# A transformer layer with windowed attention and mLSTM: values by direction, queries split in the projections, output weights loaded over items 8 to 13

## The chip, the cores and the metric

The kernel runs on one core of a Trainium2 chip. The metric is the device time of one execution in microseconds; the time of a kernel is the median of its runs. The engines are named as in the profile: PE (TensorE, with its weight loads PEld), DVE (VectorE), ACT (ScalarE), POOL (GpSimd) and SP, which issues the DMAs.

## What is computed

One layer over 1024 latent tokens of width 1024 with a prefix of 256 context tokens. Both are normed and modulated, go through one input projection, and feed two head groups: grouped attention over a band of 128 positions, all context keys and a sink, and a bidirectional mLSTM in four heads. Both are joined in one output projection; a gated feed-forward follows. Cut to its core:

```python
px = modulate(rms_norm(x, g_pre_mix), sh_m, sc_m) @ w_in
aqx, akx, avx, mqx, mkx, mvx, mox, mgx = split(px)
att_x = window_attention(rope(aqx), rope(akx), avx, kc, vc, sink)  # p = exp(s - m) * inv;  p @ v
...
num = einsum('bhts,bhsv->bhtv', s, vc) + w_inter * einsum('bhvd,bhtd->bhtv', C, qc)
den = s.sum(-1) + w_inter * einsum('bhd,bhtd->bht', n, qc)
h = num / maximum(abs(den), exp(-m_t))      # forward and backward, summed
...
mix_x = concatenate([att_x, ml_x], -1) @ w_out
x = x + gt_m * rms_norm(mix_x, g_post_mix)
x = x + gt_f * rms_norm(swiglu(modulate(rms_norm(x, g_pre_ffn), ...)), g_post_ffn)
```

## The kernel before

Matmuls that must be exact to float32 are made as three: every operand is split into a high part (a cast, on ACT) and a low part (a subtraction, on DVE or POOL), and `mm3` adds high x high, high x low and low x high. The stages stand one after the other in the trace: modulation vectors, norm and transposed tokens (0 to 162 us), projections (162 to 307), attention and mLSTM (307 to 498), output projection (to about 590) and feed-forward.

**Projections.** `TILES` lists 13 tiles of 128 output rows: mLSTM keys and queries (mk, mq), attention keys (ak), attention queries (aq0 to aq3), output gates (mo). `tproj` makes one tile with 48 matmuls of 512 columns (three accumulators where the context needs one, all of tag "mm", four banks of PSUM), and its result is evicted by `conv`, `rope` or a sigmoid while PE makes the next tile. aq tiles are stored to DRAM (`aq_d`) as float32.

**Attention and mLSTM.** There are 16 items (n, g): a block of 128 query positions and a key head. `Soft(i)` makes the scores (`scores(h)`: four matmuls into a tile of tag "s", two banks each and two of them; DVE's L780 then evicts, masks and takes the row's limit) and `norm` (exponentials on ACT, L789; a reciprocal on DVE; the scaling on POOL, L794). `Values(i)` transposes the probabilities (`tr`, L808, into a bank "pt"), splits them (`th` on ACT, `tl` on DVE) and multiplies them with the values into one bank "po" (`mm`, L818 and L819; `out` copies and adds). In items 0 to 7 block n = i of the mLSTM is made too: `ml_scores` (L693, in tag "s"), `ml_values`, `ml_norm`, `ml_out`. The two halves of a 128-row mLSTM query tile hold two heads (hb = 0 and 1). A call of `ml_values` takes one direction d and one half hb: one bank, for each of two heads a matmul of 64 rows with the state (L707) and one of 128 rows with the values (L708), then two small operations and a reciprocal on DVE (L711 to L713) and two evictions (ACT L717 for d = 0, DVE L719 for d = 1). Scores run two items ahead of values.

The strings `PLAN_ML` and `PLAN` set the order in which an item's steps are written. A scheduler then orders the instructions of each engine from that, by its own estimates, up to the last two items, which stand under a manual order. PSUM has three banks of tag "pt" and one of "po". `q_load(i)` fetches the queries of an item, `q_split` (POOL, L570 and L571) makes their high and low parts.

**Output weights.** `wout_load(j)` loads one of eight 128 x 1024 slabs of w_out, casts it on ACT (L749) and makes the low part on POOL (L750); j = 0 is made in two halves on ACT and DVE. They lie in tiles `R(k)` of a shared pool, the high part in R(2j), the low part in R(2j+1) and the raw slab in R(2j-1). `omm(n, hf, ks)` multiplies row n's split mix (`msplit`, mh and ml) with the slabs 4 hf + k; 24 matmuls for one half of a row.

Of the kernel before, what the change touches and what calls it, by code (L numbers as in the profile page):

```python
# [9 lines left out]
F32 = mybir.dt.float32  # L10
# [6 lines left out]
P = 128  # L17
# [16 lines left out]
PLAN_ML = "T0 q A0 A1 A2 A3 T1 T2 T3 M0 M1 T4 V0 N0 M2 V1 M3 M4 O z V2 w V3 s N1 x"  # L34
PLAN = "T0 q A0 A1 A2 A3 T1 T2 T3 N0 M0 T4 M1 M2 N1 M3 M4 O z l"


def body(tc, x, ctx, vecs, bcv, bada, gqm, gqf, wada, ws1, ws2, wt, wout, wfi, wfo,
# [377 lines left out]
    aq_d = tc.dram_tile([8, 64, S], F32, name="aq_d")  # L416
# [140 lines left out]
    qds, qhl, prs, wo = {}, {}, {}, {}  # L557

    def q_load(i):

        n, g = items[i]
        qd = qds[i] = qq.tile([P, 4, P], F32, name="qd", tag="qd", bufs=2)
        for d in range(2):
            dma(qd[64 * d:64 * d + 64], aq_d[4 * g:4 * g + 4, :, n * P:(n + 1) * P].rearrange("h d t -> d h t"))

    def q_split(i):
        qd = qds.pop(i)
        qh = qq.tile([P, 4, P], F32R, name="qh", tag="qh", bufs=2)
        ql = qq.tile([P, 4, P], F32R, name="ql", tag="ql", bufs=2)
        pool.tensor_scalar(qh, qd, 1.0, 1.0, MUL, MUL)  # L570
        pool.tensor_tensor(ql, qd, qh.bitcast(F32), SUB)  # L571
        qhl[i] = qh, ql
# [16 lines left out]
    for j, name in enumerate(TILES):  # L589
# [25 lines left out]
        elif name.startswith("aq"):  # L615
            t = T(0, f"aq{i}")
            rope(ps, t, 0.125)
            for g in range(2):
                dma(aq_d[4 * g + i], t[64 * g:64 * g + 64])
        else:  # L620
            t = R(14 if i == 3 else 15, "so", (S,))
            for k in range(2):
                act.activation(t[:, k * 512:(k + 1) * 512], ps[k], AF.Sigmoid)
            dve.tensor_scalar(t, t, vec[:, VGML + i:VGML + 1 + i], None, MUL)
            dma(so_d[i], t)
        if name in rest:
            ada_rest(rest[name], j + 1)
        if name == "aq3":
# [3 lines left out]
            for i in range(2):  # L632
                q_load(i)
                q_split(i)
# [28 lines left out]
    qa = atp[1]  # L663
    qa.tile([P, 80], F32, name="padq")

# [34 lines left out]
    def ml_values(n, d, hb):  # L700
        wt_, qp_, hs = wts[n], qps[n], hss[n][0]
        s_, r0 = rows_of(n, d)
        cs = state(d, s_)
        r = slice(hb * 64, hb * 64 + 64)
        pv = bank().rearrange("p a b -> p (a b)")[:, 0:258].rearrange("p (j v) -> p j v", j=2)
        for j in range(2):
            pe.matmul(pv[:, j, :], qp_[r, d, j, :], cs[r, j, :], start=True, stop=False)  # L707
            pe.matmul(pv[:, j, :], wt_[:, d, 2 * j + hb, :], V[:, n, 2 * j + hb, :], start=False, stop=True)  # L708
        dn = qa.tile([P, 2], F32, name="dn", tag="dn", bufs=8)
        den = pv[:, :, 128]  # L710
        dve.tensor_tensor(dn, den, emcol[:, r0 + hb:r0 + 4:2], MAX)  # L711
        dve.scalar_tensor_tensor(dn, den, -1.0, dn, MUL, MAX)
        dve.reciprocal(dn, dn)  # L713
        for j in range(2):
            t = hs[:, 2 * j + hb]
            if d == 0:
                act.activation(t, pv[:, j, 0:128], AF.Copy, scale=dn[:, j:j + 1])  # L717
            else:
                dve.scalar_tensor_tensor(t, pv[:, j, 0:128], dn[:, j:j + 1], t, MUL, ADD)  # L719
# [18 lines left out]
    def wout_load(j):  # L738
        h, l = R(2 * j, f"woh{j}", (D,), F32R), R(2 * j + 1, f"wol{j}", (D,), F32R)
        if j == 0:  # L740
            for i in range(2):
                sl = slice(i * 512, (i + 1) * 512)
                load_split(h[:, sl], l[:, sl], wout[j][:, sl],
                           qq.tile([P, 4, P], F32, name="wor0", tag="qd", bufs=2).rearrange("p a b -> p (a b)"))
            wo[j] = h, l
            return
        raw = R(2 * j - 1, f"wor{j}", (D,))
# [83 lines left out]
    for i in range(2):  # L831
# [5 lines left out]
        if i == 0:  # L837
            q_load(2)
            ml_scores(0)

    for i in range(NIT):
# [6 lines left out]
        for k in (PLAN_ML if i < NT else PLAN).split():  # L848
            op, n = k[0], int(k[1:] or 0)
            if op == "q" and a:  # L850
                q_split(i + 2)
            elif op == "w" and i + 1 < NT:
# [11 lines left out]
            elif op == "V" and i < NT:  # L864
                ml_values(i, n // 2, n % 2)
# [6 lines left out]
            elif op == "l" and i > NT:  # L872
                for j in {9: (7,), 10: (6,), 11: (5, 4), 12: (3, 2), 13: (1, 0)}[i]:
                    wout_load(j)

# [3 lines left out]
    ops_ = {0: pb.tile([P, 1024], F32, name="s", tag="s", bufs=2)}  # L879
    mhl = {}  # L880

    def msplit(n, hf):
        h, l = (qq.tile([P, 4, P], F32R, name=f"m{x_}{hf}", tag=f"q{x_}", bufs=2) for x_ in "hl")
        split(h, l, mix[n][:, 4 * hf:4 * hf + 4, :])
        mhl[n, hf] = h, l

    def omm(n, hf, ks):
        h, l = mhl[n, hf]
        for k in ks:
            j = 4 * hf + k  # L890
            for i in range(2):
                sl = slice(i * 512, (i + 1) * 512)
                mm3(ops_[n][:, sl], (h[:, k], l[:, k]), (wo[j][0][:, sl], wo[j][1][:, sl]), j == 4, j == 3)

# [20 lines left out]
    msplit(0, 0)  # L915
# [4 lines left out]
    omm(0, 0, range(4))  # L920
# [856 lines left out]
```

## Time and profile before

| what | us |
|---|---|
| runs | 1230.72, 1234.12, 1235.18 (median 1234.12) |
| profiled execution | 1231.71 |
| its span | 1229.9 |
| granted TensorE clock, mean | 0.996 |

Times in rows of the profile are counted from the span's start. A row of the timeline has the start, the duration, the engine, the line, the operation, out<-in with shapes and how many like it were merged; what stands in brackets is how long the engine had been idle before and what released it. Matmul rows overlap, since they are pipelined, so what one costs is the time from its start to the start of the next.

### The profile page before, as it was taken

What the parts mean: (1) busy time and instruction counts of PE and PEld (TensorE: products, weight loads), DVE (VectorE), ACT (ScalarE), POOL (GpSimd) and SP (SyncE); (2) the same over time, 40 slices, a digit from 0 to 9 for tenths busy, and PEclk for the clock granted to TensorE, in tenths of its full rate; (3) what the DMA queues carried; (4) which work ended last, traced back from release to release, by engine and by line L of the source; (5) the groups of instructions that cost most, each with busy time, mean ns of one, the idle gap of its engine ahead of it and who ended that gap; (6) DMA issues with size and microseconds to landing.
All of it is one profiled execution on the core that took longest, in us unless ns stands there. A gap on an engine that the chain in (4) does not pass through costs nothing.

```text
span 1229.9 us, 16238 instructions
## 1 busy us (share of the span) xinstructions
PE 1193.5 (97%) x5859; PEld 968.9 (79%) x5859; DVE 799.9 (65%) x1385; ACT 578.1 (47%) x1105; POOL 205.8 (17%) x245
## 2 busy tenths in 40 slices
PE   7889999999999998999999999999999999999997
PEld 1779878877777776887778888888888888888886
DVE  3882177772877788446867677767777755554567
ACT  3754533211766786587643333334333334444443
POOL 0651410235544476000000000000000000000000
PEclk9899999999999999999999999999999999999999
DMA  8542854556533320522034465575645548665853
GB/s 313 168 132 70 280 188 144 181 145 191 153 90 87 112 78 10 188 86 86 18 104 136 180 218 198 204 246 195 230 141 177 176 162 279 205 205 188 299 188 129
DMA packets 91096, 202.30 MB, mean 164 GB/s; under 512 B 9092, under 2 KB 29956, under 8 KB 89608
## 3 DMA queue, kind: packets, MB, share of 16 engines
q1 hardware_dynamic: 91016, 201.27, 49.4%
q8 instruction: 46, 0.75, 0.2%
q14 instruction: 34, 0.28, 0.1%
HBM read 149.85 MB, written 50.73 MB: 163 GB/s over the span
## 4 chain that ended last, share of the span: by engine, by line
PE 78%; DMA 7%; DVE 7%; POOL 3%; ACT 3%; issue 2%; SPq 1%; DVEq 0%; POOLq 0%; ACTq 0%
PE xv L72 8%; PE xv L70 8%; PE xv L71 8%; PE pt L70 5%; PE pt L71 5%; PE pt L72 5%; PE pt L708 2%; PE pt L707 2%; PE pt L808 2%; DMA wb<-in_wada 2%; PE op L72 2%; PE fx L70 2%; PE fx L71 2%; PE fx L72 2%; PE op L71 2%
## 5 line engine op out<-in xcount | busy, mean ns | idle before, releaser
L59 DVE TENSOR_TENSOR fo<-fr,fo 128x1024 fp32r<-128x1024 f32 x77 | 92.7, 1222 | 70.9 <-ACT fo L58 67.7
L58 ACT CAST fo<-fr 128x1024 fp32r<-128x1024 f32 x77 | 79.5, 1050 | 74.0 <-PE pt L72 34.9
L441 PE MATMUL t<-hh,th 128*128 128x512 f32 x208 | 82.5, 397 | 1.8 <-ACT cr L458 1.8
L442 PE MATMUL t<-hl,th 128*128 128x512 f32 x208 | 82.1, 395 | 0.0
L1192 ACT CAST wS<-wr 128x512 fp32r<-128x512 f32 x88 | 54.1, 622 | 55.8 <-PE pt L72 37.5
L1194 DVE TENSOR_TENSOR wS<-wr,wS 128x512 fp32r<-128x512 f32 x88 | 60.3, 688 | 20.7 <-ACT wS L1192 20.7
L444 PE MATMUL t<-hh,tl 128*128 128x512 f32 x208 | 68.2, 393 | 0.0
L70 PE MATMUL xv<-tT,wS 128*128 128x512 f32 x168 | 66.0, 393 | 0.0
L72 PE MATMUL xv<-tT,wS 128*128 128x512 f32 x168 | 65.6, 391 | 0.0
L71 PE MATMUL xv<-tT,wS 128*128 128x512 f32 x168 | 65.5, 390 | 0.0
L492 DVE SCALAR_TENSOR_TENSOR acc<-wb,csil,acc 128x1024 f32<-128x1024 f32 x24 | 33.9, 1411 | 40.6 <-DMA wb<-in_wada 40.6
L441 PEld LDWEIGHTS t<-hh,th 128*128 128x128 f32 x208 | 39.1, 188 | 10.4 <-ACT cr L458 2.4
L944 DVE TENSOR_TENSOR wr<-wr 128x512 f32<-128x512 f32 x66 | 45.5, 689 | 1.4
L442 PEld LDWEIGHTS t<-hl,th 128*128 128x128 f32 x208 | 39.1, 188 | 8.1 <-issue 1.2
L1226 ACT ACTIVATE es<-es 128x512 f32<-128x512 f32 x22 | 13.9, 633 | 66.6 <-DVE es L947 66.6
L72 PE MATMUL op<-woh,ml 128*128 128x512 f32 x112 | 43.8, 391 | 0.8 <-DVE ml L59 0.8
L444 PEld LDWEIGHTS t<-hh,tl 128*128 128x128 f32 x208 | 38.3, 188 | 7.9 <-issue 1.0
L70 PE MATMUL op<-woh,mh 128*128 128x512 f32 x112 | 44.2, 395 | 0.0
L71 PE MATMUL op<-wol,mh 128*128 128x512 f32 x112 | 43.7, 390 | 0.0
L70 PE MATMUL pt<-fo 128*128 128x512 f32 x110 | 42.8, 389 | 0.0
L71 PE MATMUL pt<-fo 128*128 128x512 f32 x110 | 42.8, 389 | 0.0
L72 PE MATMUL pt<-fo 128*128 128x512 f32 x110 | 42.8, 389 | 0.0
(991 smaller groups left out, 3489.9 us busy)
## 6 DMA issues: line engine op xcount, KB each, us to landing
wr<-in_wfi SPq DMA_DIRECT2D x44, 512.0 KB, 4.8
wb<-in_wada SPq DMA_DIRECT2D x24, 512.0 KB, 4.3
s_d<-a SPq DMA_DIRECT2D x22, 512.0 KB, 6.6
bt<-in_wfo SPq DMA_DIRECT2D x44, 256.0 KB, 3.7
tb_d<-bt SPq DMA_DIRECT2D x11, 1024.0 KB, 4.1
fr<-s_d SPq DMA_DIRECT2D x44, 256.0 KB, 4.5
fr<-tb_d SPq DMA_DIRECT2D x44, 256.0 KB, 4.3
fr<-a_d SPq DMA_DIRECT2D x33, 256.0 KB, 4.2
```

What stands on the lines that cost most here:

```text
L58: act.copy(hi, raw)
L59: dve.tensor_tensor(lo, raw, hi.bitcast(F32), SUB)
L70: pe.matmul(ps, a[0], b[0], start=first, stop=False, **kw)
L71: pe.matmul(ps, a[0], b[1], start=False, stop=False, **kw)
L72: pe.matmul(ps, a[1], b[0], start=False, stop=last, **kw)
L441: pe.matmul(o, wh[:, kt], m[0], start=f, stop=False)
L442: pe.matmul(o, wh[:, kt], m[1], start=False, stop=False)
L444: pe.matmul(o, wl[:, kt], m[0], start=False, stop=l)
L492: dve.scalar_tensor_tensor(a, t, csil[:, kt, 0:1], a, MUL, ADD)
L944: dve.tensor_tensor(out, a, b, SUB)
L1192: act.copy(w[:, 0], raw)
L1194: dve.tensor_tensor(w[:, 1], raw, w[:, 0].bitcast(F32), SUB)
```

## The change

1. Attention queries are split in the projections: each aq tile is cast on ACT and subtracted on DVE, both parts are stored (four stores and not two), and `q_load` makes four loads in place of two, with three buffers. `q_split` is gone from POOL.
2. The context accumulator of `tproj` takes a bank of tag "tp" and not a third one of "mm". In the attention stage "pt" and "po" are allocated first, so that "s" gets other banks than those that the last projection sums hold.
3. `ml_values` takes a direction, with both halves: two banks at once, four state matmuls, four value matmuls, one reciprocal.
4. `wout_load` runs j = 0 to 7 over items 8 to 13, with the raw slab in R(2j+2) (that of j = 7 in V), and all low parts on POOL.
5. `msplit(0, 0)` and `omm(0, 0, ...)` move from the end of the manual order into item 13.

```diff
-PLAN_ML = "T0 q A0 A1 A2 A3 T1 T2 T3 M0 M1 T4 V0 N0 M2 V1 M3 M4 O z V2 w V3 s N1 x"
-PLAN = "T0 q A0 A1 A2 A3 T1 T2 T3 N0 M0 T4 M1 M2 N1 M3 M4 O z l"
+PLAN_ML = "T0 A0 A1 A2 A3 T1 T2 T3 M0 M1 T4 V0 N0 M2 M3 M4 O z V1 w s N1 x"
+PLAN = "T0 A0 A1 A2 A3 T1 T2 T3 N0 M0 T4 M1 M2 N1 M3 M4 O z l"
+PLAN13 = "T0 A0 A1 A2 A3 m T1 T2 P0 T3 N0 M0 T4 M1 P1 M2 N1 M3 P2 M4 O P3 l"
+WLOADS = {8: (0, 1), 9: (2,), 10: (3,), 11: (4,), 12: (5, 6), 13: (7,)}
...
-        ps = [pa.tile([P, 512], F32, name=f"t{j}_{i}", tag="mm", bufs=4) for i in range(3 if with_ctx else 2)]
+        ps = [pa.tile([P, 512], F32, name=f"t{j}_{i}", tag="mm", bufs=4) for i in range(2)]
+        if with_ctx:
+            ps.append(pa.tile([P, 4, P], F32, name=f"tc{j}", tag="tp", bufs=2).rearrange("p a b -> p (a b)"))
...
-        pool.tensor_scalar(qh, qd, 1.0, 1.0, MUL, MUL)
-        pool.tensor_tensor(ql, qd, qh.bitcast(F32), SUB)
-        qhl[i] = qh, ql
+        qhl[i] = [qq.tile([P, 4, P], F32R, name=f"q{p}", tag=f"q{p}", bufs=3) for p in "hl"]
+        for t, src in zip(qhl[i], aq_d):
+            for d in range(2):
+                dma(t[64 * d:64 * d + 64].bitcast(F32), src[4 * g:4 * g + 4, :, n * P:(n + 1) * P].rearrange("h d t -> d h t"))
...
             rope(ps, t, 0.125)
-            for g in range(2):
-                dma(aq_d[4 * g + i], t[64 * g:64 * g + 64])
+            qp2 = R(3, f"aqh{i}", (S,), F32R), t.bitcast(F32R)
+            split(*qp2, t)
+            for d, o in zip(aq_d, qp2):
+                for g in range(2):
+                    dma(d[4 * g + i], o[64 * g:64 * g + 64].bitcast(F32))
...
+    for x_, n in (("pt", 3), ("po", 1)):
+        pb.tile([P, 4, P], F32, name=x_, tag=x_, bufs=n)
...
-    def ml_values(n, d, hb):
+    def ml_values(n, d):
...
-        pv = bank().rearrange("p a b -> p (a b)")[:, 0:258].rearrange("p (j v) -> p j v", j=2)
+        pv = [bank().rearrange("p a b -> p (a b)")[:, 0:258].rearrange("p (j v) -> p j v", j=2) for hb in range(2)]
         for j in range(2):
-            pe.matmul(pv[:, j, :], qp_[r, d, j, :], cs[r, j, :], start=True, stop=False)
-            pe.matmul(pv[:, j, :], wt_[:, d, 2 * j + hb, :], V[:, n, 2 * j + hb, :], start=False, stop=True)
...
+            for hb in range(2):
+                r = slice(hb * 64, hb * 64 + 64)
+                pe.matmul(pv[hb][:, j, :], qp_[r, d, j, :], cs[r, j, :], start=j == 0, stop=False,
+                          skip_group_check=j > 0)
+        for hb in range(2):
+            for j in range(2):
+                pe.matmul(pv[hb][:, j, :], wt_[:, d, 2 * j + hb, :], V[:, n, 2 * j + hb, :], start=False, stop=True,
+                          skip_group_check=j > 0)
...
-        raw = R(2 * j - 1, f"wor{j}", (D,))
+        raw = R(2 * j + 2, f"wor{j}", (D,)) if j < 7 else V.rearrange("p n h v -> p (n h v)")[:, 0:D]
...
+            elif op == "m":
+                msplit(0, 0)
+                ops_[0] = pb.tile([P, 1024], F32, name="op", tag="s", bufs=2)
+            elif op == "P":
+                omm(0, 0, range(n, n + 1))
...
-    msplit(0, 0)
...
-    omm(0, 0, range(4))
```

How this stands on the engines after the scheduler, at three places. Lines after the change are a few higher: L707 and L708 are L711 and L715, L808 is L811, L818 and L819 are L821 and L822, L570/L571 have no successor, L794 is L797.

PE, the values of one direction of an mLSTM item, before (pt is a bank, cs the state, qp the queries, wl the weighted scores):

```order
L707 MATMUL pt_3579<-cs2_2339,qp4_3453 128x129
L708 MATMUL pt_3579<-V_87,wl4_3451 128x129
L707 MATMUL pt_3579<-cs2_2339,qp4_3453 128x129
L708 MATMUL pt_3579<-V_87,wl4_3451 128x129
L819 MATMUL po_3498<-tl__3554,av2_90 128x512
L818 MATMUL po_3498<-th__3562,av2_90 128x512
L707 MATMUL pt_3597<-cs2_2339,qp4_3453 128x129
L708 MATMUL pt_3597<-V_87,wl4_3451 128x129
```

The same place after the change, an item on:

```order
L821 MATMUL po_3680<-th__3734,av2_90 128x512
L711 MATMUL pt_3760<-cs2_2358,qp5_3646 128x129 x2
L715 MATMUL pt_3760<-V_87,wl5_3644 128x129 x2
L822 MATMUL po_3680<-tl__3735,av2_90 128x512
L821 MATMUL po_3680<-th__3743,av2_90 128x512
L711 MATMUL pt_3761<-cs2_2358,qp5_3646 128x129 x2
L715 MATMUL pt_3761<-V_87,wl5_3644 128x129 x2
L822 MATMUL po_3680<-tl__3744,av2_90 128x512
```

Within a bank the two state matmuls now stand together and the two value matmuls too. The banks of the two halves are not interleaved, though the code writes them so: the scheduler has put each bank's four matmuls in one place.

POOL, at the start of the attention stage, before (pr are the probabilities of an item, its first column filled from the sinks in bcr):

```order
L767 COPY pr__2799<-bcr 128x4
L570 TENSOR_SCALAR qh<-qd 128x512
L571 TENSOR_TENSOR ql<-qd,qh 128x512
L794 TENSOR_SCALAR pr__2713<-pr__2713,sm 128x512 x4
L570 TENSOR_SCALAR qh<-qd 128x512
L571 TENSOR_TENSOR ql<-qd,qh 128x512
L794 TENSOR_SCALAR pr__2762<-pr__2762,sm 128x512 x2
```

And after:

```order
L770 COPY pr__2788<-bcr 128x4
L770 COPY pr__2825<-bcr 128x4
L797 TENSOR_SCALAR pr__2736<-pr__2736,sm 128x512 x4
L797 TENSOR_SCALAR pr__2788<-pr__2788,sm 128x512 x2
L770 COPY pr__2984<-bcr 128x4
```

Nothing stands between the copies of the sinks and the first scaling any more.

PE, at the end of the manual order, before (s holds the first row of the output projection here, mh and ml are the split mix, woh and wol the output weights):

```order
L818 MATMUL po<-th__4990,av_90 128x512
L819 MATMUL po<-tl__4991,av_90 128x512
L70 MATMUL s<-woh_4866,mh_4981 128x512
L71 MATMUL s<-wol_4867,mh_4981 128x512
L72 MATMUL s<-woh_4866,ml_4982 128x512
```

These rows go on to 24 matmuls. After the change, item 13 has this, with the same matmuls under the name op:

```order
L822 MATMUL po<-tl__4716,av_90 128x512
L811 MATMUL pt<-cst,pr__4525 128x128 x4
L72 MATMUL op<-woh_4297,mh_4784 128x512
L73 MATMUL op<-wol_4298,mh_4784 128x512
L74 MATMUL op<-woh_4297,ml_4785 128x512
```

22 of the 24 follow each other there, ahead of six transposes of pr__4525, and the last two come eight rows later. Behind the last L822 of the program the second row of the output projection follows at once.

More of the change, by code (lines that the diff above doesn't have):

```diff
@@ L839, in body, with msplit, omm @@
             ml_scores(0)
+    ops_, mhl = {}, {}
+    def msplit(n, hf):
+        h, l = (qq.tile([P, 4, P], F32R, name=f"m{x_}{hf}", tag=f"q{x_}", bufs=3) for x_ in "hl")
+        split(h, l, mix[n][:, 4 * hf:4 * hf + 4, :])
+        mhl[n, hf] = h, l
+    def omm(n, hf, ks):
+        h, l = mhl[n, hf]
+        first, last = (0, 7) if n == 0 else (4, 3)
+        for k in ks:
+            j = 4 * hf + k
+            for i in range(2):
+                sl = slice(i * 512, (i + 1) * 512)
+                mm3(ops_[n][:, sl], (h[:, k], l[:, k]), (wo[j][0][:, sl], wo[j][1][:, sl]), j == first, j == last)
     for i in range(NIT):
@@ L847, in body @@
             break
[L848 removed]
+        for k in (PLAN_ML if i < NT else PLAN13 if i == NIT - 3 else PLAN).split():
             op, n = k[0], int(k[1:] or 0)
[L850 to L852 removed]
+            if op == "w" and i + 1 < NT:
                 ml_load(i + 1)
```

63 lines of the change are left out of this document (19 added, 44 removed).

## Prediction

> **What bounds the kernel now.** I read the page first, for which engine the chain of waits runs over, then the windows by stage, then single rows of the stages that the change touches.
>
> ```profile
> span 1229.9 us, 16238 instructions
> PE 1193.5 (97%) x5859; PEld 968.9 (79%) x5859; DVE 799.9 (65%) x1385; ACT 578.1 (47%) x1105; POOL 205.8 (17%) x245
> ...
> PE 78%; DMA 7%; DVE 7%; POOL 3%; ACT 3%; issue 2%; SPq 1%; DVEq 0%; POOLq 0%; ACTq 0%
> ```
>
> TensorE is busy in all but 36 us of the span, and the chain that ended last is mostly PE. So a change can gain only by giving PE fewer or cheaper instructions, or by taking its few waits. The windows say where other engines are near too (PE, PEld, DVE, ACT, POOL busy, each with its count):
>
> ```profile
> 162.00:307.00 145.00, 143.24 (x763) 114.79 (x761) 91.89 (x132) 33.00 (x48) 40.58 (x60) 1.00 0.55 164
> 307.00:322.00 15.00, 12.21 (x82) 10.04 (x80) 12.45 (x34) 12.12 (x27) 7.99 (x11) 1.00 0.68 223
> 353.00:368.00 15.00, 14.94 (x90) 11.72 (x90) 11.29 (x38) 9.55 (x28) 6.21 (x8) 1.00 0.32 88
> 440.00:484.00 44.00, 39.69 (x250) 33.09 (x251) 40.54 (x88) 38.59 (x88) 36.79 (x39) 1.00 0.11 31
> ```
>
> The projections (162 to 307) and a middle mLSTM item (353 to 368, about one item) are PE alone: DVE has 3.7 us of 15 free. Items 8 to 13 (about 440 to 484) are shared by four engines. Out projection and feed-forward, from 504 on, are not changed, so a gain before them passes to the end whole. The sum below is made against the profiled execution's own 1231.71 us (span 1229.9); the median of the three runs is 1234.12, 2.4 more.
>
> **Values by direction.** This is the largest term, and only the shape of PE's rows makes it. One call of before issues a 64-row state matmul, a 128-row V matmul, and both again (a merged row of x2 is one matmul of the program, in two passes):
>
> ```profile
> 354.32 0.49 PE L707 MATMUL pt<-cs,qp 64*128 64x129 f32 x2
> 354.73 0.49 PE L708 MATMUL pt<-V,wl 128*128 128x129 f32 x2
> 355.15 0.49 PE L707 MATMUL pt<-cs,qp 64*128 64x129 f32 x2
> 355.57 0.49 PE L708 MATMUL pt<-V,wl 128*128 128x129 f32 x2
> 355.81 0.47 PE L819 MATMUL po<-tl__3201,av 128*128 128x512 f32 x1
> ```
>
> From start to start an L707 or L708 takes 0.42 us while a matmul of the other shape follows, and the last L708 takes 0.24 us, since L819 has 128 rows too. The 0.18 us between is what a change of row count costs. The weight loads show it: the load below begins at 354.73, with its own matmul and not ahead of it, whereas between equal shapes the load of L778 begins at 356.13, 0.22 ahead of its matmul at 356.35.
>
> ```profile
> 354.73 0.30 PEld L708 LDWEIGHTS pt<-V,wl 128*128 128x128 f32 x2
> ...
> 356.13 0.19 PEld L778 LDWEIGHTS s<-k,qh 128*128 128x128 f32 x1
> ```
>
> A call has 4 such changes (into L707, to L708, back, to L708). The order after has, for each bank, two 64-row and then two 128-row matmuls: 2 changes. So 2 x 0.18 = 0.36 us a call, and 2 directions x 2 halves x 8 items = 32 calls: 11.5 us of PE's slots. It is not all taken off: item 0 runs beside other waits (PE 12.2 of 15 in 307 to 322), and DVE, ACT and the wait for the scores set some moments once PE is faster. I take five sixths, **-9.6 us**. The bounds are 0 and 13.
>
> The code alternates the row halves (hb 0, 1, 0, 1), and before has rows that show such pairs:
>
> ```profile
> 325.26 0.72 PE L693 MATMUL s<-mq,mk 64*128 64x128 f32 x8
> 325.91 0.44 PE L778 MATMUL s<-k,qh 128*128 128x384 f32 x1
> ```
>
> Four matmuls of alternating halves take 0.65 us, 0.16 each. But the order after puts a bank's four matmuls together, so the two 64-row ones that are neighbours are of one half. I count nothing for pairs.
>
> DVE loses one reciprocal per direction (0.15 us), 0.3 an item; POOL loses two instructions per item. Neither engine binds there, so I count zero. The price of it is in the rivals: a direction's results are read only when both banks are full.
>
> **Projections.** The third accumulator of the context tiles leaves the four "mm" banks. This is the one wait it removes; ACT still evicts mk0's sum when mk1 wants a bank:
>
> ```profile
> 164.31 0.50 PE L441 MATMUL t<-hh,th 128*128 128x512 f32 x1 [1.76 <-ACT cr L458]
> ...
> L58 ACT CAST fo<-fr 128x1024 fp32r<-128x1024 f32 x77 | 79.5, 1050 | 74.0 <-PE pt L72 34.9
> L59 DVE TENSOR_TENSOR fo<-fr,fo 128x1024 fp32r<-128x1024 f32 x77 | 92.7, 1222 | 70.9 <-ACT fo L58 67.7
> ```
>
> The "tp" banks are idle by then. The window had 143.24 of 145.00 us of PE busy, and this wait is the whole rest, so 1.76 us go: **-1.8**. Added: four splits of aq, each a cast (1.05 by the L58 row) and a subtraction (1.22), 4.2 us on ACT and 4.9 on DVE in 145 us, where ACT has 33.0 and DVE 91.9; and 8 more stores and 2 more loads per item on SP. PE hides them, unless an eviction that PE needs is queued behind a split; then up to 2.3 us (1.05 + 1.22) come back. I take 0.
>
> **Start of attention.** Scores no longer take the banks that the last projection sum holds, and POOL no longer splits queries ahead of the first norm:
>
> ```profile
> 308.27 0.75 DVE L624 TENSOR_SCALAR so<-so,vec 128x1024 f32<-128x1024 f32 x1 [6.56 <-ACT so L623]
> 308.38 0.36 PE L778 MATMUL s<-k,qh 128*128 128x256 f32 x1 [1.04 <-ACT so L623]
> ...
> 309.24 0.75 DVE L780 CUSTOM_DVE_ANT_0 pr__2713<-s,mask,bcr 128x512 f32<-128x512 f32 x1 [0.21 <-DMA wl<-w_dr]
> ...
> 311.44 0.62 POOL L570 TENSOR_SCALAR qh<-qd 128x512 fp32r<-128x512 f32 x1 [7.20 <-PE s L778]
> 312.14 1.28 POOL L571 TENSOR_TENSOR ql<-qd,qh 128x512 fp32r<-128x512 f32 x1
> ...
> 314.15 0.55 PE L808 MATMUL pt<-cst,pr__2713 128*128 128x128 f32 x3 [1.03 <-POOL pr__2713 L794]
> ```
>
> The wait of 1.04 goes, but DVE's `so` at 308.27, which still needs that sum's sigmoid, stands ahead of the first L780, so little of it is won: 0.2. The transposes at 314.15 wait 1.03 for a norm that could not begin before 313.42, because two split instructions held POOL from 311.44. They go; DVE's row sums are next, so I take 0.7 of the 1.03. Together **-0.9** (bounds -2.1 and 0).
>
> **Items 8 to 13.** Before, ACT's casts of output weights run early; four of seven whole ones and two halves of 0.62 lie after 427, now all eight:
>
> ```profile
> L749 ACT CAST woh<-wor x7: 1043/1045/1047, 413.8 to 451.1; 128x1024 fp32r<-128x1024 f32 x7
> ...
> L571 POOL TENSOR_TENSOR ql<-qd,qh 128x512 fp32r<-128x512 f32 x3 | 3.9, 1304 | 0.1
> L750 POOL TENSOR_TENSOR wol<-wor,woh 128x1024 fp32r<-128x1024 f32 x7 | 16.8, 2404 | 0.7 <-PE pt L707 0.7
> ```
>
> That is 4 x 1.05 - 1.2, and 0.6 for the moved cast of mh: 3.6 us more on ACT, which has 38.6 of 44. POOL gives up its splits and takes one more L750 of 2.4. Each cast waits for the L750 ahead of it, as h_j lies in raw_j-1; behind a waiting cast on ACT stand the exponentials and the casts of p, and PE waits for those. Bounds 0 and 3.6; I take **+1**.
>
> **End of the stage.** PE's waits between 470 and 490 are these:
>
> ```profile
> PE po L819 <- DVE tl__4825 L59: 1.2, 1, 1.2
> PE po L819 <- DVE tl__4729 L59: 0.8, 1, 0.8
> PE pt L808 <- DVE tl__4807 L59: 0.8, 1, 0.8
> PE po L818 <- DVE mix L827: 0.7, 1, 0.7
> PE s L70 <- ACT mh L58: 0.5, 1, 0.5
> ...
> 497.95 0.39 PE L819 MATMUL po<-tl__4991,av 128*128 128x512 f32 x1
> 498.18 0.39 PE L70 MATMUL s<-woh,mh 128*128 128x512 f32 x1
> ...
> 498.38 0.58 ACT L826 COPY o<-po 64x512 f32<-64x512 f32 x1 [1.73 <-PE po L819]
> 498.98 1.14 ACT L58 CAST mh<-mix 128x512 fp32r<-128x512 f32 x2
> ...
> 503.62 0.39 PE L70 MATMUL op<-woh,mh 128*128 128x512 f32 x1
> ```
>
> The waits are 4.0 us in all. The 24 matmuls of omm(0, 0) now fill 498.18 to 503.62, 0.227 us each. The order after sets them into item 13, 22 of them as one lump of 5 us ahead of its last transposes, and DVE no longer does j=0's low part; I count 3.5 us of the waits covered. In the tail they covered the last copy: the last po matmul ends at 498.34, o takes to 498.96 and the first mh half of 1.14, so PE would go on at 499.6 and not at 498.2. That is 1.4, and with mix and ml, which DVE makes behind the same copy, I estimate 1.8 given back: **-1.7** (bounds -4 and +1).
>
> **Sum.** -1.8 - 0.9 - 9.6 + 1.0 - 1.7 = -13.0: 1218.7 from the profiled execution, 1221.1 from the median. I put down 1220.0, between the two.
>
> **Rivals.** (1) Only half is won, since another thing binds as soon as PE's slots shrink. For it: DVE has 11.3 of 15 us in an item, so it would be at 11 of 13.8, with every L711 still behind PE; ACT is nearly full in items 8 to 13. Against it: PE was busy for 14.94 of the 15 us, so nothing bound beside it yet. Half of 9.6 and all of the 3.6: 1218.7 + 4.8 + 2.6 = 1226.1, 1228.5 from the median. The same 4.8 would be lost if two 64-row loads of one half did not hide behind each other (0.18 of the 0.36 a call): 1223.5; no row of before has that pair.
>
> [...]
>
> (2) Pairs run side by side after all. Per direction that makes the four state matmuls 0.65 for 0.96 and leaves 2 changes of shape for 4, and with the exit it is about 0.85 us; 16 directions x 0.85 x 5/6 = 11 more: 1207.4. Against it stands the order of the banks.
>
> (3) Slower: held banks. Two of the three pt banks belong to a direction until DVE and ACT have read both. Before, the last L708 ends near 356.06 and a bank came free only after these:
>
> ```profile
> 356.09 0.16 DVE L711 TENSOR_TENSOR dn<-pt,emcol 128x2 f32<-128x2 f32 x1 [1.57 <-PE pt L708]
> 356.66 1.15 ACT L717 ACTIVATE hs<-pt,dn 128x128 f32<-128x128 f32 x4 [1.78 <-PE pt L708]
> ```
>
> That is to 357.81, about 1.75 us. If PE stood through it in each of 16 directions, with the scores (1.2 us) covering it in half of them, it would lose 8 x 1.75 + 8 x 0.55 = 18.4 and, with 13.0 won, end at 1237.1; and with no cover at 1246.7. It outweighs the gain from 0.8 us a direction. I price it at 1242. Against it: a third bank is left, and items have some 10 us outside the values for five transposed tiles.
>
> **How the numbers follow.** Forecast 0.60 (1213 to 1227), half won 0.25 (1223 to 1231), pairs 0.07 (1207), slower 0.08 (1242). About 0.5%, 6 us, is what a measurement here tells from no change. Below 1228 lie the forecast, the pairs and two fifths of the half: 0.77; above 1240 0.08; between 0.15. The range 1207 to 1232 leaves out the slower case and some tail.
>
> **What would show it.** Middle items 1.0 to 1.5 us shorter, with 1.13 us from a bank's first state matmul to the row behind its values (354.32 to 355.81, 1.49, now); no wait of PE at the second tile of the projections; the norm row of POOL straight behind DVE's row sums; PE waits in items 8 to 12 no longer than now; a wait of some 1.8 us ahead of the second out-projection row. PE waits of over 0.8 us for bank releases behind the values would prove me wrong.

## The result and the profile after

| | before | after |
|---|---|---|
| median of the runs, us | 1232.57 (4 runs, 1230.72 to 1235.18) | 1223.89 (4 runs, 1222.57 to 1225.44) |
| profiled execution, us | 1231.71 | 1222.57 |
| its span, us | 1229.9 | 1220.3 |

The ratio is 0.9934, with a 95% interval of 0.9915 to 0.9954: 8.7 us less by the medians, 9.1 by the profiled executions. The forecast was 13.0 less. The page of the changed kernel, with the lines that answer to those of before:

```profile
span 1220.3 us, 16269 instructions
PE 1180.1 (97%) x5859; PEld 963.3 (79%) x5859; DVE 802.7 (66%) x1371; ACT 580.8 (48%) x1108; POOL 177.1 (15%) x214
...
PE 75%; DVE 10%; ACT 5%; DMA 5%; issue 3%; POOL 2%; SPq 0%; DVEq 0%; ACTq 0%; POOLq 0%
```

PE lost 13.4 us of busy time, but the span fell by only 9.6. The chain has less PE and more DVE and ACT in it (10 and 5%, after 7 and 3%): new waits took a part back. The waits of PE from the projections to the end of attention, in all, how often, and the longest:

```profile
PE pu L549 <- DVE mkc L545: 2.6, 2, 2.2
PE s L781 <- DVE sm L783: 2.5, 4, 1.5
PE op L72 <- ACT mh L60: 1.8, 2, 1.3
PE pt L811 <- DVE tl__4682 L61: 1.5, 1, 1.5
PE pt L811 <- DVE hs L729: 1.3, 3, 0.5
PE pt L811 <- DVE tl__4574 L61: 1.2, 1, 1.2
PE ar L506 <- PE t L446: 1.0, 1, 1.0
```

The first, the one of 1.5 in the second (it stands at the start of attention, where two of 1.0 stood before), the 1.3 in the third, those behind tl__4682 and tl__4574 and the last are new. To see which stage won and lost, I cut each profiled execution at the same PE rows: the first and last matmul of the projections, the first and last state matmul of the values, the first matmul of the output projection's second row, and the last matmul of the program.

| stage, us | before | after | forecast of the difference | measured |
|---|---|---|---|---|
| up to the first projection matmul | 132.7 | 131.1 | 0 | -1.6 |
| projections | 174.2 | 176.9 | -1.8 | +2.7 |
| start of attention | 14.3 | 12.7 | -0.9 | -1.5 |
| first to last state matmul | 116.7 | 105.9 | -9.6 | -10.8 |
| items 8 to 15, to the second row | 65.7 | 67.3 | +1.0 - 1.7 = -0.7 | +1.6 |
| the rest | 719.8 | 719.8 | 0 | 0.0 |

The first line is no effect of the change: in the kernels of the experiments the same stage takes 130.6 to 132.5 us. The 24 moved matmuls lie in the fifth stage in both kernels. The cuts do not fall on quite the same work, though: after the change the start of attention holds four matmuls of scores fewer, 0.5 to 0.6 us, and items 8 to 15 four more, and one value matmul, 0.2 us, has gone from the stretch of the values to the stage behind it. Like for like the start of attention is about 1.0 us shorter, the values 10.6, and items 8 to 15 about 0.8 longer.

### The profile page after: what moved, and what is told of

Same layout as the page of the kernel before. It is cut to its first block, busy times and chain, and to the rows that moved or that the text cites. A ratio compares the mean times of both kernels' runs of the same rounds, so it can differ in the third digit from the quotient of the medians.

```text
span 1220.3 us, 16269 instructions
## 1 busy us (share of the span) xinstructions
PE 1180.1 (97%) x5859; PEld 963.3 (79%) x5859; DVE 802.7 (66%) x1371; ACT 580.8 (48%) x1108; POOL 177.1 (15%) x214
## 4 chain that ended last, share of the span: by engine, by line
PE 75%; DVE 10%; ACT 5%; DMA 5%; issue 3%; POOL 2%; SPq 0%; DVEq 0%; ACTq 0%; POOLq 0%
PE xv L74 8%; PE xv L72 8%; PE xv L73 8%; PE pt L73 6%; PE pt L74 6%; PE pt L72 6%; DMA wb<-in_wada 2%; PE op L74 2%; PE op L72 2%; PE op L73 2%; PE fx L72 2%; PE fx L74 2%; PE fx L73 2%; PE t L448 1%; PE t L446 1%
## 5 line engine op out<-in xcount | busy, mean ns | idle before, releaser
L448 PE MATMUL t<-hh,tl 128*128 128x512 f32 x208 | 65.4, 394 | 0.0
L72 PE MATMUL op<-woh,mh 128*128 128x512 f32 x128 | 51.1, 399 | 1.8 <-ACT mh L60 1.8
L74 PE MATMUL op<-woh,ml 128*128 128x512 f32 x128 | 50.3, 393 | 0.9 <-DVE ml L61 0.8
L73 PE MATMUL op<-wol,mh 128*128 128x512 f32 x128 | 49.9, 390 | 0.0
L781 PE MATMUL s<-k,qh 128*128 128x256 f32 (+1 forms) x128 | 40.9, 329 | 2.6 <-DVE sm L783 2.5
L72 PE MATMUL pt<-fo 128*128 128x512 f32 x110 | 42.8, 389 | 0.0
L73 PE MATMUL pt<-fo 128*128 128x512 f32 x110 | 42.8, 389 | 0.0
```

Of the source, the lines that this page charges most:

```text
L72: pe.matmul(ps, a[0], b[0], start=first, stop=False, **kw)
L73: pe.matmul(ps, a[0], b[1], start=False, stop=False, **kw)
L74: pe.matmul(ps, a[1], b[0], start=False, stop=last, **kw)
L448: pe.matmul(o, wl[:, kt], m[0], start=False, stop=l)
L781: pe.matmul(o, qh[:, h, :], k2[g][:, kc], start=True, stop=False)
```

## Experiments

Each kernel differs from the changed kernel by the edit named, unless it says otherwise. The stages of their profiled executions are in this table; the last column is explained at the end of this section. Ratios are against runs of the kernel before on the same chip.

| kernel | projections | start | values | items 8 to 15 | lost to half clock | median us | ratio (95%) |
|---|---|---|---|---|---|---|---|
| before | 174.2 | 14.3 | 116.7 | 65.7 | 0 | 1232.6 | 1 |
| changed | 176.9 | 12.7 | 105.9 | 67.3 | 0 | 1223.9 | 0.9934 (0.9915 to 0.9954) |
| values_alone | 176.1 | 14.3 | 108.0 | 73.1 | 5.1 | 1229.1 | 0.9976 (0.9962 to 0.9990) |
| split_undone | 177.5 | 16.2 | 106.2 | 68.6 | 6.8 | 1228.8 | 0.9980 (0.9968 to 0.9992) |
| weights_undone | 179.2 | 12.7 | 109.4 | 67.3 | 3.4 | 1228.5 | 0.9979 (0.9966 to 0.9992) |
| tail_undone | 177.9 | 13.6 | 105.9 | 67.9 | 5.1 | 1224.9 | 0.9938 (0.9917 to 0.9959) |
| tc_undone | 175.7 | 12.7 | 105.6 | 68.9 | 1.7 | 1221.8 | 0.9921 (0.9903 to 0.9939) |
| wb3 | 174.1 | 16.0 | 105.6 | 67.3 | 1.7 | 1220.2 | 0.9903 (0.9881 to 0.9925) |
| pairs_kept | 178.9 | 12.7 | 99.6 | 67.8 | 1.7 | 1219.3 | 0.9899 (0.9880 to 0.9918) |
| pairs_wb3 | 174.5 | 12.7 | 99.3 | 67.7 | 0 | 1214.4 | 0.9860 (0.9843 to 0.9878) |
| last_late | 174.2 | 13.6 | 99.3 | 72.2 | 5.1 | 1218.2 | 0.9882 (0.9850 to 0.9913) |
| msplit_late | 174.3 | 12.7 | 99.3 | 69.2 | 1.7 | 1213.5 | 0.9847 (0.9820 to 0.9874) |
| both_late | 175.5 | 13.5 | 99.3 | 69.4 | 1.7 | 1217.4 | 0.9875 (0.9849 to 0.9901) |

### The values alone, and what follows them

`values_alone` is the kernel before with the new `ml_values` and nothing else.

```diff
-PLAN_ML = "T0 q A0 A1 A2 A3 T1 T2 T3 M0 M1 T4 V0 N0 M2 V1 M3 M4 O z V2 w V3 s N1 x"
+PLAN_ML = "T0 q A0 A1 A2 A3 T1 T2 T3 M0 M1 T4 V0 N0 M2 M3 M4 O z V1 w s N1 x"
...
-                ml_values(i, n // 2, n % 2)
+                ml_values(i, n)
```

> The kernel before, with only the values by direction (two banks at once, state matmuls together, one reciprocal); queries, banks, weights and tail as before. Before, first state matmul to last was 116.7 us (321.2 to 437.9), in the changed kernel 105.9. Theory (fewer changes of row count on PE): the stretch falls by 10 to 11 us by this part alone, to 106 or 107, and the time by 8 to 11 us. Rival (part of the gain comes from POOL's freed time and the other banks): the stretch stays above 109 and the time falls by 4 to 7 us.

The stretch fell by 8.7 us, to 108.0: less than the theory had and more than the rival. To see what the change of order does by itself, I took each PE row of the stretch for the time from its start to the start of the next, and counted how often a matmul of 64 rows follows one of 128 or the reverse:

| kernel | changes of row count | state and value matmuls, us | all other rows with their waits, us |
|---|---|---|---|
| before | 140 | 49.5 | 67.2 |
| values_alone | 76 | 36.9 | 71.0 |
| changed | 66 | 35.7 | 70.2 |
| pairs_kept | 54 | 27.5 | 72.1 |

The 64 changes of the prediction are gone in values_alone, and the matmuls of the values are 12.6 us cheaper, so the theory on PE's rows holds. But 3.8 us came back in the other rows and their waits, among them two of 0.7 and 1.1 us for casts of probabilities (th) on ACT between 417 and 423. The changed kernel saves ten changes more, since the scheduler set the 64-row matmuls of the mLSTM scores next to the state matmuls there.

The time fell by only 3.0 us, below both forecasts. The stretch after the values grew from 65.7 to 73.1, and 3.4 us of that are a spell at half clock, of which more below. PE's waits between 425 and 490 us in this kernel are, the largest first:

```profile
PE po L825 <- DVE mix L834: 3.2, 1, 3.2
PE pt L815 <- DVE tl__4775 L59: 1.9, 1, 1.9
PE pt L815 <- DVE tl__4548 L59: 1.1, 1, 1.1
```

Before, the waits there were 1.2 at most. The items with mLSTM became shorter, and POOL still has the query splits and seven slabs of output weights to make before the end, DVE the eighth: POOL is busy for 5.00 us of 470 to 475, and then DVE for 4.81 of 475 to 480, while PE waits.

`weights_undone` takes the loading of before into the changed kernel (j from 7 down to 0 in items 9 to 13, the raw slab in R(2j-1), j = 0 on ACT and DVE), with the old tail.

```diff
-        raw = R(2 * j + 2, f"wor{j}", (D,)) if j < 7 else V.rearrange("p n h v -> p (n h v)")[:, 0:D]
+        raw = R(2 * j - 1, f"wor{j}", (D,))
...
-                for j in WLOADS[i]:
+                for j in {9: (7,), 10: (6,), 11: (5, 4), 12: (3, 2), 13: (1, 0)}[i]:
```

> The changed kernel with the output weights loaded as before (items 9 to 13, j from 7 down, j = 0 in halves on DVE) and, since they then come too late for item 13, the tail as before too. With values alone the stretch from the last state matmul to the second out-projection row took 73.1 us against 65.7 before and 67.3 after the change. Theory (the order of the weights is what keeps the gain of the values from being given back there): the stretch is 71 to 74 us and the time 3 to 6 us above the changed kernel. Rival (the freed POOL time of the query split keeps it): 66 to 69 us, time within 1.5 us of the changed kernel.

The time went as the theory said (4.6 us above the changed kernel by the medians, 5.5 by the ratios) and the place did not. Items 8 to 15 take 67.3 us as in the changed kernel; the values take 3.5 more, of which about 0.6 are four matmuls of scores that fall on the other side of the cut. The 3.4 us lost to half clock lie at 198 to 205 us, in the projections, far ahead of anything that this edit changes. So the profile shows PE waiting for ACT and DVE among the last mLSTM items, where the casts of the weights run early again; it does not show that these make the whole 4.6 us. The last of these waits lies in the stretch of the values, the other two 2 and 4 us behind its end:

```profile
PE pt L818 <- DVE hs L729: 1.1, 1, 1.1
PE po L828 <- ACT th__4204 L60: 1.0, 1, 1.0
PE po L828 <- ACT th__4044 L60: 0.7, 1, 0.7
```

`split_undone` stores aq unsplit again and puts `q_split` back on POOL.

```diff
-            qp2 = R(3, f"aqh{i}", (S,), F32R), t.bitcast(F32R)
-            split(*qp2, t)
-            for d, o in zip(aq_d, qp2):
-                for g in range(2):
-                    dma(d[4 * g + i], o[64 * g:64 * g + 64].bitcast(F32))
+            for g in range(2):
+                dma(aq_d[4 * g + i], t[64 * g:64 * g + 64])
...
+        pool.tensor_scalar(qh, qd, 1.0, 1.0, MUL, MUL)
+        pool.tensor_tensor(ql, qd, qh.bitcast(F32), SUB)
```

> The changed kernel with the query split back on POOL (aq stored once, two stores and two loads each). Theory (the new PE waits of 4.0 us between 224 and 261, put down to DVE, come from the eight more stores on SP and the splits, which make DVE's modulation sums and the state steps behind them late): no PE wait over 0.3 us between 165 and 307, the last projection matmul about 4 us earlier against the first one (172 in place of 176 us), 1 to 1.5 us given back at the first norm and some on POOL in items 8 to 13: 1 to 3 us faster than the changed kernel. Rival (the waits come with the context bank, which lets PE run ahead): the waits stay and the time is the changed kernel's or up to 2 us above.

The theory is wrong and the rival holds: the wait near 247 stays, and is longer. The same view of this kernel:

```profile
PE pu L549 <- DVE mkc L545: 3.1, 1, 3.1
...
PE pt L816 <- DVE tl__4673 L61: 1.3, 1, 1.3
PE pt L816 <- DVE tl__4564 L61: 0.9, 1, 0.9
...
PE po L826 <- ACT th__4581 L60: 0.7, 1, 0.7
PE pt L816 <- POOL pr__2717 L802: 0.6, 1, 0.6
```

So the extra stores and splits do not make the wait in the projections. The split is worth 4.9 us by the medians (5.7 by the ratios), more than the 0.9 that the prediction gave to the whole start: POOL's split ahead of the first norm costs a wait of 0.6, items 8 to 15 get 1.3 longer, and most of the rest in the profiled execution is 6.8 us lost to half clock, which the runs of this kernel share (granted clock 0.990 to 0.993, where the changed kernel had 0.994 to 0.997).

### The projections

The rows around the new wait, DVE and PE:

```profile
245.57 1.28 DVE L496 SCALAR_TENSOR_TENSOR acc<-wb,csil,acc 128x1024 f32<-128x1024 f32 x1 [2.48 <-DMA wb<-in_wada]
246.77 0.75 DVE L545 TENSOR_TENSOR mkc<-pk,wkcol 128x256 f32<-128x256 f32 x2
247.24 1.10 PE L549 MATMUL pu<-V,mkc 128*64 128x129 f32 x16 [2.22 <-DVE mkc L545]
```

DVE sums the remaining modulation weights, slab by slab, beside the projections. Here it waits 2.48 us for a slab, the scaled keys of a state step (mkc) stand behind that sum, and PE waits for the keys. In the kernel before DVE waited for its slab too, and PE did not wait for the keys:

```profile
245.27 0.74 DVE L541 TENSOR_TENSOR mkc<-pk,wkcol 128x256 f32<-128x256 f32 x2
247.93 1.10 PE L545 MATMUL pu<-V,mkc 128*64 128x129 f32 x16
```

Counted from the first projection matmul, PE comes to this step at 115.2 us before and at 113.9 in the changed kernel (247.24 less the wait), 1.3 earlier. The keys are begun at 112.6 and at 115.7, 3.1 later. So the later keys are the larger part. In the changed kernel the scheduler has set the rows of this stage in another order, on DVE, POOL and PE, and DVE's sums are late long before the keys. POOL clears the next accumulator (acc) at 62.6 us of the stage before, straight behind the PE rows that read the old one, and at 68.2 after, behind other work of its own; DVE's next sum begins at 65.8 and at 69.2. Before, then after:

```profile
195.36 0.96 POOL L485 MEMSET acc<- 128x1024 f32 x1 [6.96 <-PE ar L508]
198.52 1.28 DVE L492 SCALAR_TENSOR_TENSOR acc<-wb,csil,acc 128x1024 f32<-128x1024 f32 x1
```

```profile
199.29 0.95 POOL L489 MEMSET acc<- 128x1024 f32 x1
200.28 1.28 DVE L496 SCALAR_TENSOR_TENSOR acc<-wb,csil,acc 128x1024 f32<-128x1024 f32 x1 [2.61 <-POOL acc L489]
```

How much of the 3.1 us comes from here, and how much from the waits on DVE in between, no kernel separates. Two kernels test what the bank and the buffers have to do with it. `tc_undone` gives the context accumulator its old bank:

```diff
-        ps = [pa.tile([P, 512], F32, name=f"t{j}_{i}", tag="mm", bufs=4) for i in range(2)]
-        if with_ctx:
-            ps.append(pa.tile([P, 4, P], F32, name=f"tc{j}", tag="tp", bufs=2).rearrange("p a b -> p (a b)"))
+        ps = [pa.tile([P, 512], F32, name=f"t{j}_{i}", tag="mm", bufs=4) for i in range(3 if with_ctx else 2)]
```

> The changed kernel with the context accumulator back in a third mm bank. Theory (the wait of 1.76 us was cover for DVE: PE now comes 1.8 us or more earlier to the state steps, whose keys stand on DVE behind modulation sums that wait for their weight slabs): the wait of about 1.8 us at the second tile is back, the one near 247 us shrinks from 2.2 to under 1 us, and the projections take 175 to 177 us as in the changed kernel (176.9); time within 1.5 us of the changed kernel. Rival (the context bank is worth its 1.8 us and the waits near 247 have another cause): the waits near 247 stay and the time is 1.5 to 2.5 us above.

And `wb3` gives the slabs a third buffer:

```diff
-                t = T((1, 3)[kt % 2], f"wb{sec}_{kt}")
+                t = T((1, 3, 4)[kt % 3], f"wb{sec}_{kt}")
```

> The changed kernel with three buffers in place of two for the slabs of the modulation weights in the projections. Theory (DVE's sums wait for a slab that can be fetched only when a buffer of two is free, and the keys of a state step wait behind them on DVE): DVE's waits on the slabs between 200 and 262 fall from 5.5 to under 2.5 us, PE's wait of 2.2 us near 247 goes, the projections take 173 to 175 us and the time falls by 2 to 3 us. Rival (SP's stores or the memory set when slabs land): nothing moves by over 1 us.

PE's waits in the projections with the old bank:

```profile
PE t L443 <- ACT cr L460: 1.6, 1, 1.6
PE ar L504 <- PE t L443: 0.8, 1, 0.8
PE pu L547 <- DVE gr L505: 0.5, 1, 0.5
```

and with three buffers, DVE's longest wait between 200 and 262, and PE's:

```profile
DVE acc L496 <- DMA wb<-in_wada: 2.7, 1, 2.7
```

```profile
PE ar L506 <- issue: 1.1, 1, 1.1
PE pu L549 <- DVE gr L507: 0.9, 1, 0.9
```

With the old bank 1.6 us are back, the wait of 2.2 is gone, and the time is 1.6 us below the changed kernel's by the ratios, just past the 1.5 of the theory but inside their intervals. In this kernel the sums start as early as before (the clearing of acc stands at 62.5 us of the stage), so the order of the rows is back with the bank. With a third buffer both waits are gone, the projections take 174.1 us, and the time is 3.8 us less by the ratios (0.9903 against 0.9934), more than the theory had. DVE's waits for slabs fall from 5.5 to 2.7 us, not to under 2.5, and its wait for POOL falls too, from 2.6 to 0.6, so the buffer is not the only thing that moved. The bank taken alone is thus worth nothing or less. With the third buffer the stage is as long as before and not 1.8 us shorter, as two waits of 1.1 and 0.9 us are there instead; what the bank is worth beside three buffers no kernel shows.

### The pairs of row halves

The scheduler had not kept the written order. `pairs_kept` holds it, each matmul issued behind the one before, the second half first:

```diff
+        prev = None
         for j in range(2):
-            for hb in range(2):
+            for hb in (1, 0):
...
+                with tc.issue_after(prev.ins):
+                    prev = pe.matmul(pv[hb][:, j, :], qp_[r, d, j, :], cs[r, j, :], **kw)
```

> The changed kernel with the state matmuls of a direction held in the written order of alternating row halves (each issued behind the one before). Theory A (two matmuls of different halves run side by side in two banks, as the scores L693 do): three or four state matmuls stand at 0.16 us each in place of 0.24 to 0.3; 0.3 to 0.6 us a direction, so 4 to 9 us off. Theory B (another thing than PE's slots already binds in the items): pairs seen starting within 20 ns, but the stretch of the values shrinks by under 2 us. Theory C: no pair starts together.

Theory A holds. First the changed kernel's values of one half, then the second part of a direction here:

```profile
364.68 0.71 PE L711 MATMUL pt<-cs,qp 64*128 64x129 f32 x4
365.32 0.71 PE L715 MATMUL pt<-V,wl 128*128 128x129 f32 x4
365.79 0.48 PE L822 MATMUL po<-tl__3383,av 128*128 128x512 f32 x1
```

```profile
363.89 0.71 PE L717 MATMUL pt<-cs,qp 64*128 64x129 f32 x6
364.53 1.16 PE L721 MATMUL pt<-V,wl 128*128 128x129 f32 x8
365.45 0.48 PE L828 MATMUL po<-tl__3392,av 128*128 128x512 f32 x1
```

Six records, three matmuls, now take the 0.64 us that four records took; the first two start 6 ns apart. The values shrank by 6.3 us, 0.39 a direction; 0.4 of that are two value matmuls that fall behind the cut here. `pairs_wb3` has pairs and the third buffer.

> Pairs of row halves kept, and three slab buffers. If both gains stand for themselves: 1217 us or less (1219.3 with pairs alone, less 2 to 3). If the projections do not gain: 1219 to 1220.

Both gains stand for themselves: 1214.4 us, 1.4% below the kernel before (0.9860), which beats both kernels of this case.

### The end of the stage

`tail_undone` puts `msplit(0, 0)` and the 24 matmuls back where they were.

```diff
     mm_t(b2, 0, 1)
+    msplit(0, 0)
     b2.tr(3)
...
     b2.out()
+    omm(0, 0, range(4))
```

> The changed kernel with msplit(0, 0) and the 24 matmuls of omm(0, 0) back at the end of the manual order. Prediction on record: the move is worth 1.7 us, so this is 1 to 3 us slower than the changed kernel, with PE waits of 3 us or more in items 12 and 13. Rival (the move gains nothing, since the waits in items 12 and 13 come from ACT's weight casts ahead of the casts of the probabilities and only change their place, and 1.8 us open behind the last copy): within 1 us of the changed kernel, or faster.

The rival holds: 0.9938 against 0.9934 is no difference. The waits of 1.2 and 1.5 us behind tl__4574 and tl__4682 are in items 12 and 13, ahead of the lump, and the lump cannot cover them. tail_undone has them too, as 0.6 and 1.5. Behind them its largest wait up to the second row is 0.5 us: the waits of before between 470 and 490 are gone without the lump as well, so it is not the lump that removed them. ACT's rows ahead of the second show what makes it:

```profile
462.14 1.05 ACT L752 CAST woh<-V 128x1024 fp32r<-128x1024 f32 x1
463.07 0.61 ACT L60 CAST th__4681<-pt 128x512 fp32r<-128x512 f32 x1
```

A slab's cast stands ahead of the cast of probabilities that frees the bank. At the other end the last copy lies open:

```profile
492.28 0.39 PE L822 MATMUL po<-tl__4987,av 128*128 128x512 f32 x1
492.70 0.58 ACT L829 COPY o<-po 64x512 f32<-64x512 f32 x1 [1.73 <-PE po L822]
493.31 1.14 ACT L60 CAST mh<-mix 128x512 fp32r<-128x512 f32 x2
...
493.98 0.50 PE L72 MATMUL op<-woh,mh 128*128 128x512 f32 x1 [1.31 <-ACT mh L60]
```

Three more kernels are built on pairs_wb3, and two of them move one of the suspects each: `last_late` loads the eighth slab under the manual order, ahead of `msplit(0, 1)`; `msplit_late` holds msplit(0, 0) behind an exponential of item 13 and puts it after N0; `both_late` does both.

```diff
-WLOADS = {8: (0, 1), 9: (2,), 10: (3,), 11: (4,), 12: (5, 6), 13: (7,)}
+WLOADS = {8: (0, 1), 9: (2,), 10: (3,), 11: (4,), 12: (5, 6), 13: ()}
...
     b.tr(1)
+    wout_load(7)
     msplit(0, 1)
```

```diff
-PLAN13 = "T0 A0 A1 A2 A3 m T1 T2 P0 T3 N0 M0 T4 M1 P1 M2 N1 M3 P2 M4 O P3 l"
+PLAN13 = "T0 A0 A1 A2 A3 T1 T2 T3 N0 m P0 M0 T4 M1 P1 M2 N1 M3 P2 M4 O P3 l"
...
-                msplit(0, 0)
+                with tc.issue_after(a.e.ins):
+                    msplit(0, 0)
```

Here `a.e` is the last exponential of Soft(15) that is written by then, that of N0's second head.

> Pairs kept and three slab buffers, and the eighth slab of the output weights (cast on ACT, low part on POOL) loaded under the manual order of item 14, not in item 13. In the kernel with both gains PE waits 1.48 us at 455.6 for a low part of probabilities, whose high part stands on ACT behind that cast of 1.05 us. Theory (ACT's weight casts ahead of the casts of the probabilities make the waits in items 12 and 13): this wait falls to under 0.6 us, and from the last state matmul to the second out-projection row it takes 66.2 to 67.2 us in place of 67.7. Rival (POOL or DVE set that moment): the wait stays over 1 us or moves by a few us with the same length.

> Pairs kept and three slab buffers, and msplit(0, 0), which the scheduler had put into item 12, held behind an exponential of item 13. Theory: the wait of 1.16 us at 446.9, behind mh's cast (0.63 on ACT) and ml's subtraction (1.15 on DVE), falls to under 0.6 us; the stretch to the second out-projection row is 66.5 to 67.4 us in place of 67.7. Rival: the wait stays, or one of the same length comes before the 24 matmuls.

> The last two edits together: if both waits go and none comes in their place, 65 to 66.2 us for the stretch (67.7 without them), and a time of 1212 to 1213.5 us.

In pairs_wb3 the two waits were 1.5 and 1.2. In last_late, then in msplit_late, PE's waits between 425 and 480 are:

```profile
PE op L74 <- DVE ml L61: 1.7, 1, 1.7
PE op L72 <- ACT mh L60: 1.5, 1, 1.5
PE pt L817 <- DVE tl__4574 L61: 1.2, 1, 1.2
PE pt L817 <- DVE tl__4682 L61: 0.5, 1, 0.5
```

```profile
PE pt L817 <- DVE tl__4682 L61: 1.5, 1, 1.5
PE pt L817 <- DVE tl__4574 L61: 0.6, 1, 0.6
```

Each edit takes the wait that it was aimed at, 1.5 to 0.5 and 1.2 to 0.6 (0.64, where under 0.6 was forecast), so the two causes are shown. Neither keeps its gain as forecast. In last_late the slab that is cast later stands ahead of mh: PE's wait for mh grows from 0.5 to 1.5, and a wait of 1.7 for ml is new, since its subtraction takes 2.44 us on DVE while POOL makes the slab's low part (in the changed kernel such a row took 1.15 us beside a low part on POOL, and 0.68 or 0.69 with POOL idle). The kernel is 3.8 us slower than pairs_wb3; its profile has 5.1 us lost to half clock, 3.4 of them at these two waits. msplit_late's stretch grew by 1.4 with a spell at half clock of 1.7 in it, and by the medians it is even with pairs_wb3 (1213.5 and 1214.4, intervals overlapping). both_late missed its forecast: the two waits are 0.6 and 0.5, but the new ones of 1.5 and 1.7 are there, the stretch takes 69.4 us and the time is 1217.4.

### What the waits cost beyond their length

In ten of the thirteen profiles the granted clock falls to one half in these four stages, for 3.4 or 6.8 us, behind a wait of PE or inside one. In values_alone, the last column but two being the clock:

```profile
475.00:480.00 5.00, 0.82 (x5) 0.59 (x6) 4.81 (x5) 1.33 (x3) 3.05 (x5) 0.84 0.01 2
480.00:485.00 5.00, 5.00 (x17) 4.01 (x17) 2.46 (x4) 1.76 (x3) 0.00 (x0) 0.50 0.00 0
```

I summed (1 - clock) over 1 us windows in the four stages of the table. The sums are 0, 1.7, 3.4, 5.1 and 6.8 us, whole multiples of 1.71: spells of 3.41 us at half speed. The profiled executions of before and after have none in these stages, so their difference is not made by it; some of the variants lose 2 to 7 us to it.

The other runs of a kernel have no profile, but each has its mean granted clock. (1 - clock) times the time, averaged over the runs, is an estimate of what a kernel loses to a lower clock over its whole length, if PE sets the pace while it lasts:

| kernel | lost, us (estimate) |
|---|---|
| before, on two chips | 6.1 and 5.5 |
| changed | 5.8 |
| values_alone | 9.1 |
| split_undone | 10.1 |
| weights_undone | 10.0 |
| pairs_wb3 | 5.5 |
| last_late | 9.1 |
| both_late | 7.6 |

By it, 4.3 of the 4.9 us that split_undone loses against the changed kernel are time at a lower clock, 4.2 of the 4.6 of weights_undone, and 3.6 of the 3.8 by which last_late is behind pairs_wb3; values_alone would have gained 6.0 us and not 3.0.

## Why the prediction was right, and where it was not

The time, 1223.9, lies in the range and the sign is right; 13.0 us were forecast and 8.7 came. The range of 1207 to 1232 is wide, and 1223.9 lies in the stretch of the rival with half the gain (1223 to 1231) too. Something of its mechanism came: waits on ACT and DVE took back a part of what PE won. By its steps:

- **Values: right in mechanism; near in size by two misses that cancel.** 1.13 us were forecast from a bank's first state matmul to the row behind its values; the rows at 364.68 and 365.79 give 1.11. Before and after, this is the whole of the group of state matmuls, with the shortest, the median and the longest in ns and the first and last start:

```profile
L707 PE MATMUL pt<-cs,qp x128: 272/323/375, 321.2 to 437.9; 64*128 64x129 f32 x128
```

```profile
L711 PE MATMUL pt<-cs,qp x128: 269/272/375, 320.8 to 426.6; 64*128 64x129 f32 x128
```

  From one middle item to the next it took 15.25 us before, 13.85 with the values alone (the 1.44 of the forecast, 1.4 measured) and 13.67 after. The rows of the values gave 13.8 us where the prediction had 11.5, as 74 changes went and not 64 and each was worth a little more; 3.0 came back in the other rows and their waits, where it had allowed 1.9. That the stretch gave 10.8 for 9.6 is thus partly luck. The rival of an open second load is refuted, since it would have made 1.31 of the 1.11: of the two matmuls of one row half in this bank, the load of the second begins at 364.89, 0.11 ahead of its matmul (365.00) and during the first, which ends at 365.17. Of held banks only short waits show (behind hs, 0.6 at the longest): the slower rival did not come.
- **Pairs.** That the scheduler's order would not make them was read rightly from the order of the engines, and pairs_kept shows what was missed: some 5.8 us in the stage like for like, where the rival had 11.
- **Projections: the step that failed.** "So 1.76 us go: -1.8" supposed that PE, once let go, runs on unhindered to 307, with the other engines as they were. PE came 1.3 us earlier to a state step whose keys DVE, in another order of rows, made 3.1 us later. The stage took 2.7 us more: 4.0 us of new waits less the 1.8, and 0.5 in other rows. That the bank brings it is shown, since tc_undone takes it back; through which row on DVE it comes stays open. The sentence on the splits and stores ("I take 0") was right for this stage: split_undone has the same wait.
- **Start of attention: near.** The table has -1.5 for -0.9, and like for like it is about -1.0. The waits went another way: the two of 1.0 us are gone whole, and one of 1.5 us behind DVE's row limits (sm) has come.
- **Items 8 to 13: the place and cause right, the size not.** +1 was taken between 0 and 3.6; slab casts and mh made two waits of 1.2 and 1.5, 2.6 together.
- **End: the term that came to nothing.** 3.5 us of waits were to be covered by the lump; they are gone, but in tail_undone they are gone without it, and 2.6 stand ahead of it instead. The 1.8 given back was near: from the last po matmul to the next row took 1.70 in place of 0.23. Together with the step above, -0.7 became +1.6 (about +0.8 like for like).
- **What the sum left out** is the clock. The values alone are worth 3.0 us in time for 8.7 in their stage; without the weights' new order or without the query split the changed kernel loses 4.6 and 4.9. By the estimate above, most of the last two and 3.0 us of the first are time at a lower clock. Whether a wait sets a spell off, and which, and why these three kernels have more of them, stays open, since each kernel has one profile.

## What to carry to other kernels

Where PE alternates matmuls of 64 and 128 rows (0.18 us a change here), group those of one shape, and hold those of different row halves next to each other by an explicit order if a scheduler regroups them by bank (some 5.8 us here). Before a wait is counted as a gain, follow what the engine meets next: here the removed wait of 1.76 us had stood beside a chain of transfers and sums on another engine, the scheduler set that chain in another order when the bank changed, and a wait of 2.22 came behind it. When a variant is slower than its stages explain, compare the granted clock of its runs before looking for a cause in its edit: here, by the estimate from the clocks, that was most of the difference in three variants (4.3 of 4.9, 4.2 of 4.6 and 3.6 of 3.8 us).

## Not expected of the hardware

The thirteen profiles have 84 PE waits of 0.7 to 3.2 us in the four stages and 16 spells at half the granted clock, about one to five; a spell lasts 3.41 us, or twice that, and each 3.41 costs 1.71 by the sum above; for example 0.70 us at 224.5 in tail_undone and 1.03 us at 225.4 in pairs_kept were followed by one, while 2.22 us at 247.2 in the changed kernel was not. Thirteen of the spells begin 0.1 to 3.1 us behind the end of a wait, three inside one.
